# Zero-padding short matrix products to 128 rows in two attention blocks and a decay branch

## The chip, the cores and the metric

The kernel runs on one core of one Trainium2 chip. The metric is the device time of one execution in microseconds. The kernel before takes 2192.56 us, the median of three runs (2187.98 to 2196.63).

A core has a matrix engine (TensorE, PE in the profile; its weight loads have a row of their own, PEld), a vector engine (VectorE, DVE), an engine for activation functions and copies (ScalarE, ACT), GpSimd (POOL), and a queue engine (SyncE, SP) that issues the transfers. A matrix product takes a stationary operand (the weights, loaded first) and a moving one. Both lie with the contracted index on up to 128 partitions; "rows" below are these partitions. In the profile's `64*128 64x512`, 64 rows are contracted into 128 outputs, for 512 columns.

## The reference, cut to what matters

Two transformer blocks run over 256 tokens of width 1024. Each has a mixing part and an expert part (PEER: every token picks experts by two lists of 128 keys, and the kernel computes all 16384 of them densely and weighs them). The mixing part of the first block is windowed attention (8 query heads of 64 over 2 key heads, with 256 context tokens) beside a short convolution:

```
s_loc = einsum('bnqhgd,bnkhd->bhgnqk', qb, kb) * scale
s_ctx = einsum('bnqhgd,bchd->bhgnqc', qb, k_ctx) * scale
p = softmax(concatenate([s_loc, s_ctx, sink_l]))
```

The second block puts 16 meta tokens before the 256. It has latent attention, whose scores are the sum of a part of 128 dimensions and a rotary part of 64, and beside it a gated linear attention with a decay for each key dimension:

```
s = einsum('bqhd,bkhd->bhqk', qn, k_nope) + einsum('bqhd,bkd->bhqk', qp, k_pe)   # 128 and 64 dimensions
out = einsum('bhqk,bkhd->bqhd', w, v)                                           # keys: 256 tokens and 16 meta
log_a = log_sigmoid(ga @ w_a2 + b_a) / 16                                       # ga: rank 16
o = decayed causal attention of gq, gk, gv over the same 272 positions
```

## The kernel before, in words

Activations lie transposed, features on the partitions and tokens in the columns. A large product is computed in three passes (`mm3`, L177 to L179) of operands split into a high and a low part (type F32R): high by high, low by high, high by low. The 512 KB weight tiles come in one stream in the order of use: SyncE loads a raw tile (L48), ScalarE casts it to the high part (L67), VectorE subtracts to the low part (L70), TensorE uses both. Small products of attention and norms take plain F32 operands; the trace shows each as two passes ("x2").

The order is that of the Python code. Short pieces of work are generators; each time a weight tile's product has been written, every generator goes one step further, so the pieces of an attention unit stand between the plain products, a tile or more apart. Each engine runs its own list in order and waits on semaphores of the others.

The products that the change touches are these. Block 1's `attend` (L522, eight units of 128 queries, two key heads each): the scores' first product (L526) has 128 rows, the query's high part in one half of the partitions and its low part in the other, against the key's high part in both; the second (L527) takes the 64 rows of the query's high part against the key's low part `kl`. Block 2's `attend` (L1368, eight heads): each of three score blocks (272, 16 and 128 columns) is a product of 128 rows (L1377) and one of 64 (L1378); then the values are summed over keys in products of 128 rows (L1413), and over a third chunk of 48 rows that holds the meta tokens (L1414). `gla_head` (L1498, four heads): products of 128 rows (L1502, L1504) and between them one of 16 for the meta tokens (L1503). `decay` (L1263, four heads): one product of 16 rows with `wa2` (L1267).

Buffers come from pools; a tile with a tag shares its buffers with the others of the tag in turn. Opening block 2's pool reuses the memory of the expert stage before it.

Of the kernel before, what the change touches and what calls it, by code (L numbers as in the profile page):

```python
# [21 lines left out]
T = 256  # L22
META = 16
# [95 lines left out]
class Build:  # L119
# [215 lines left out]
    def block1_pre(self):  # L335
        tc, nc, A, const, spawn = self.tc, self.nc, self.A, self.const, self.spawn
        with ExitStack() as es:
# [114 lines left out]
            kh = pool.tile([128, 2, 2 * T], F32R, name="kh")  # L452
            kl = pool.tile([128, 2 * T], F32R, name="kl")
            both = ((0, slice(0, 64), slice(64, 128)), (1, slice(64, 128), slice(0, 64)))
            kT = pool.tile([128, T], F32, name="kT")
            vT = pool.tile([128, 2 * T], F32, name="vT")
            v = pool.tile([128, 4, 128], F32, name="v")
# [31 lines left out]
            def key(half, k):  # L489
                ks = slice(half * T, half * T + T)  # L490
                if not half:
                    yield from rotate(kT, k)
                    k = kT
                    yield
                for g, own, other in both:
                    nc.scalar.copy(kh[own, g, ks], k[own])
                    nc.scalar.copy(kh[other, g, ks], k[own])
                yield
                for g, own, other in both:
                    nc.vector.tensor_sub(kl[own, ks], k[own], kh[own, g, ks].bitcast(F32))  # L500

# [20 lines left out]
            def attend(b, qt):  # L522
                ts = slice(qt * 128, qt * 128 + 128)
                S = ps.tile([128, 2, 512], F32, name="S", tag="S", bufs=1)
                for g, own, other in both:
                    nc.tensor.matmul(S[:, g, :], qs[:, b, g, ts], kh[:, g, :], start=True, stop=False)  # L526
                    nc.tensor.matmul(S[:, g, :], qs[own, b, g, ts], kl[own, :], start=False, stop=True)  # L527
                yield
# [622 lines left out]
    def block2_pre(self):  # L1151
        tc, nc, A, const, spawn = self.tc, self.nc, self.A, self.const, self.spawn
        with ExitStack() as es:
# [7 lines left out]
            nh = pool.tile([128, KC, L2], F32R, name="nh")  # L1161
            nl = pool.tile([128, KC, L2], F32R, name="nl")
            wa2 = pool.tile([128, 512], F32, name="wa2")
            nc.sync.dma_start(wa2[64:80, :], A["w_a2"])
            rope = self.load("rope2", pool)
# [90 lines left out]
            kp = pool.tile([128, L2], F32, name="kp")  # L1256
            kpe = pool.tile([128, L2], F32, name="kpe")
            la = pool.tile([128, 4 * L2], F32, name="la")
# [4 lines left out]
            def decay():  # L1263

                for h in range(4):
                    pl = bank("pla", "hd")
                    nc.tensor.matmul(pl[:, :L2], wa2[64:80, h * 128:h * 128 + 128], kp[64:80, :], start=True, stop=True)  # L1267
                    yield
                    nc.scalar.activation(lat[:, h, :], pl[:, :T], AF.Identity, bias=gb_a[:, h:h + 1])
                    nc.scalar.activation(lam[:, h, :], pl[:, T:L2], AF.Identity, bias=gb_a[:, h:h + 1])  # L1270
                    yield
                for a in range(0, 4 * L2, 2 * L2):
                    a, b = la[:, a:a + 2 * L2], lb[:, a:a + 2 * L2]
                    nc.vector.scalar_tensor_tensor(b, a, -1.0, a, op0=ALU.mult, op1=ALU.min)
                    yield
                    nc.scalar.activation(b, b, AF.Exp)
                    yield
                    nc.scalar.activation(b, b, AF.Ln, bias=1.0)
                    yield
                    nc.vector.scalar_tensor_tensor(a, a, 0.0, b, op0=ALU.min, op1=ALU.subtract)  # L1280
                    nc.vector.tensor_scalar(a, a, 1.0 / 16, None, op0=ALU.mult)
                ready[0] = True
# [22 lines left out]
            def key_rope(s):  # L1305

                p = bank("pkd", "hd"), bank("pkr", "mm", 3)
                nc.tensor.matmul(p[0][:, :L2], dup[:64, :], s, start=True, stop=True)
                nc.tensor.matmul(p[1][:, :L2], rotd, s, start=True, stop=True)
                yield  # L1310
                t = pool.tile([128, L2], F32, name="kr", tag="rh", bufs=3)
                nc.vector.tensor_mul(kpe, p[0][:, :L2], rope[:, 0, :])
                nc.vector.tensor_mul(t, p[1][:, :L2], rope[:, 1, :])
                nc.vector.tensor_add(kpe, kpe, t)

# [37 lines left out]
            nc.scalar.copy(kp, mm("kpe", 0, nh, nl, L2))  # L1353
            s1 = pool.tile([64, L2], F32, name="s1")

# [7 lines left out]

            PMs = [pool.tile([48, 2, 128], F32, name="PM%d" % q) for q in range(2)]
            for t in PMs:
                nc.vector.memset(t, 0.0)

            def attend(h):  # L1368


                gs = slice(h % 2 * 64, h % 2 * 64 + 64)
                parts = (slice(288, 432), slice(0, 272))
                S = bank("S2", "S", 2)
                for q, o, ks in ((1, slice(0, 272), slice(0, L2)), (0, slice(288, 304), slice(T, L2)),
                                 (0, slice(304, 432), slice(0, 128))):
                    qs = slice(q * 128, q * 128 + 128)
                    nc.tensor.matmul(S[:, o], qT[:, h, qs], kT[:, h, ks], start=True, stop=False)  # L1377
                    nc.tensor.matmul(S[:, o], qT[gs, 8 + h // 2, qs], kpe[gs, ks], start=False, stop=True)  # L1378
                yield
# [30 lines left out]
                for q, chunks in ((0, ((0, 0),)), (1, ((0, 1), (1, 2)))):  # L1410
                    oq = o[:, q * 128:q * 128 + 128]
                    for j, (c, w) in enumerate(chunks):
                        nc.tensor.matmul(oq, v[:, c, hs], PT[:, w, :], start=j == 0, stop=False)  # L1413
                    nc.tensor.matmul(oq, v[:48, 2, hs], PM[:, q, :], start=False, stop=True)  # L1414
                yield
# [5 lines left out]
                           for a, b in ((0, 1024), (1024, 1536), (1536, 2560)))  # L1421
            AM = AM[:META]
            own = (AT[:, :, 0:128], AT1)
# [17 lines left out]
            def gla():  # L1441

                for tt in range(2):
                    nc.vector.memset(own[tt], 0.0)
                while not ready[0]:
                    yield
# [37 lines left out]
                for hp in range(2):  # L1484
                    nc.scalar.copy(AM[:, 2 * hp:2 * hp + 2, :], p[hp])
                while left[0]:
# [11 lines left out]
            def gla_head(h, o, bh):  # L1498
                p = bank("pgo", "S", 2).rearrange("p (e t) -> p e t", e=2)
                for e in range(2):  # L1500
                    vs = slice(h * 256 + e * 128, h * 256 + e * 128 + 128)
                    nc.tensor.matmul(p[:, e, :], gv[:, 0, vs], AT[:, h, :], start=True, stop=False)  # L1502
                    nc.tensor.matmul(p[:, e, :], gv[:META, 2, vs], AM[:, h, :], start=False, stop=False)  # L1503
                    nc.tensor.matmul(p[:, e, 128:], gv[:, 1, vs], AT1[:, h, :], start=False, stop=True)  # L1504
# [26 lines left out]
            for n, (kind, i) in enumerate(self.mixed):  # L1531
# [19 lines left out]
                elif kind == "ukv":  # L1551
                    if i == 0:
                        kT = pool.tile([128, 8, L2], F32, name="kT2")
                        v = pool.tile([128, 3, 1024], F32, name="v2")
                    for j in range(4 * i, 4 * i + 4):
                        p = mm("ukv", j, ckh, ckl, L2, 2, 4)
# [180 lines left out]
```

## Time and profile before

| | |
|---|---|
| median of three runs | 2192.56 us |
| profiled execution, its own time | 2196.02 us |
| its span, first to last instruction | 2194.0 us |
| TensorE busy | 2156.2 us (98%), 15318 products |
| weight loads busy | 1970.3 us (90%) |
| VectorE busy | 1585.6 us (72%) |
| ScalarE busy | 1289.5 us (59%) |
| GpSimd busy | 0.2 us, 4 instructions |
| transfers | 386.49 MB, mean 176 GB/s |
| mean granted TensorE clock | 0.997 of full speed |

The two mixing parts take 0 to 250 and about 1050 to 1395 us, the two expert parts the rest. Products are pipelined and their ends are modelled, so that durations overlap: the time that a product costs is the distance from its start to the start of the next one. A busy TensorE is therefore not a TensorE at its peak, and the table alone does not tell it.

### The profile page before, as it was taken

What the parts mean: (1) busy time and instruction counts of PE and PEld (TensorE: products, weight loads), DVE (VectorE), ACT (ScalarE), POOL (GpSimd) and SP (SyncE); (2) the same over time, 40 slices, a digit from 0 to 9 for tenths busy, and PEclk for the clock granted to TensorE, in tenths of its full rate; (3) what the DMA queues carried; (4) which work ended last, traced back from release to release, by engine and by line L of the source; (5) the groups of instructions that cost most, each with busy time, mean ns of one, the idle gap of its engine ahead of it and who ended that gap; (6) DMA issues with size and microseconds to landing.
All of it is one profiled execution on the core that took longest, in us unless ns stands there. A gap on an engine that the chain in (4) does not pass through costs nothing.

```text
span 2194.0 us, 39324 instructions
## 1 busy us (share of the span) xinstructions
PE 2156.2 (98%) x15318; PEld 1970.3 (90%) x15318; DVE 1585.6 (72%) x3063; ACT 1289.5 (59%) x2480; POOL 0.2 (0%) x4
## 2 busy tenths in 40 slices
PE   6999999999999999999999999999999999999999
PEld 3999899999999888888888889999999999888887
DVE  5786699988887555665775546699988897555555
ACT  6565554568887444444675456554568886544443
POOL 0000000000000000000000000000000000000000
PEclk9999999999999999999999999999999999999999
DMA  8576656655555666776443235566665556666665
GB/s 261 156 246 194 197 170 184 188 178 156 158 159 170 188 193 194 214 232 204 153 131 96 87 116 164 158 178 197 182 178 160 155 156 181 186 194 195 193 192 154
DMA packets 108155, 386.49 MB, mean 176 GB/s; under 512 B 12784, under 2 KB 14128, under 8 KB 107712
## 3 DMA queue, kind: packets, MB, share of 16 engines
q1 hardware_dynamic: 107968, 383.98, 58.0%
q8 instruction: 120, 1.97, 0.4%
q14 instruction: 67, 0.55, 0.1%
HBM read 382.88 MB, written 1.05 MB: 175 GB/s over the span
## 4 chain that ended last, share of the span: by engine, by line
PE 92%; DVE 3%; ACT 3%; DMA 1%; issue 1%; SPq 0%; ACTq 0%; DVEq 0%
PE acc L730 32%; PE pu L177 12%; PE pu L179 12%; PE pu L178 12%; PE pz L177 5%; PE pz L179 4%; PE pz L178 4%; PE pg L1029 3%; DVE wlo L70 1%; ACT whi L67 1%; PE pa L1433 1%; PE sp L1077 1%; PE po L565 1%; PE S L1378 1%; PE pu L224 1%
## 5 line engine op out<-in xcount | busy, mean ns | idle before, releaser
L70 DVE TENSOR_TENSOR wlo<-raw,whi 128x1024 fp32r<-128x1024 f32 x690 | 841.4, 1220 | 439.5 <-ACT whi L67 434.8
L67 ACT CAST whi<-raw 128x1024 fp32r<-128x1024 f32 x690 | 722.6, 1048 | 404.4 <-PE acc L730 347.7
L177 PE MATMUL pu<-hh,whi 128*128 128x256 f32 x2272 | 649.3, 286 | 0.0
L179 PE MATMUL pu<-hh,wlo 128*128 128x256 f32 x2272 | 635.9, 280 | 0.3
L178 PE MATMUL pu<-hl,whi 128*128 128x256 f32 x2272 | 635.6, 280 | 0.0
L178 PEld LDWEIGHTS pu<-hl,whi 128*128 128x128 f32 x2272 | 431.2, 190 | 0.0
L179 PEld LDWEIGHTS pu<-hh,wlo 128*128 128x128 f32 x2272 | 429.1, 189 | 1.1 <-DVE wlo L70 1.1
L177 PEld LDWEIGHTS pu<-hh,whi 128*128 128x128 f32 x2272 | 426.7, 188 | 0.0
L730 PE MATMUL acc<-whi,ch 128*128 128x512 f32 x1024 | 317.2, 390 | 0.0
L730 PE MATMUL acc<-whi,cl 128*128 128x512 f32 x1024 | 316.7, 389 | 0.0
L730 PE MATMUL acc<-wlo,ch 128*128 128x512 f32 x1024 | 316.6, 389 | 0.0
L730 PEld LDWEIGHTS acc<-whi,cl 128*128 128x128 f32 x1024 | 192.2, 188 | 40.1
L730 PEld LDWEIGHTS acc<-wlo,ch 128*128 128x128 f32 x1024 | 192.2, 188 | 39.8
L730 PEld LDWEIGHTS acc<-whi,ch 128*128 128x128 f32 x1024 | 191.6, 188 | 39.3
L1116 ACT ACTIVATE cb<-pu 128x256 f32<-128x256 f32 (+32 forms) x250 | 81.9, 328 | 163.6 <-PE pu L179 163.4
L1013 ACT ACTIVATE w<-oi,lists 128x128 f16<-128x128 f16 x512 | 170.3, 442 | 1.9 <-DVE oi L1007 1.4
L1021 DVE TENSOR_TENSOR cb<-cb,pg 128x248 f32<-128x248 f32 (+42 forms) x128 | 69.7, 544 | 60.7 <-ACT cb L1116 60.7
L706 DVE TENSOR_TENSOR cl<-cb,ch 128x256 fp32r<-128x256 f32 x256 | 96.6, 419 | 5.2 <-ACT ch L704 5.2
L177 PE MATMUL pz<-nh,whi 128*128 128x256 f32 (+1 forms) x328 | 97.0, 296 | 0.0
L179 PE MATMUL pz<-nh,wlo 128*128 128x256 f32 (+1 forms) x328 | 93.2, 284 | 0.0
L178 PE MATMUL pz<-nl,whi 128*128 128x256 f32 (+1 forms) x328 | 92.9, 283 | 0.0
L1114 ACT ACTIVATE gl<-pu 128x4 f32<-128x4 f32 (+21 forms) x132 | 37.3, 283 | 79.6 <-ACT w L1013 67.3
(420 smaller groups left out, 2892.9 us busy)
## 6 DMA issues: line engine op xcount, KB each, us to landing
raw<-u SPq DMA_DIRECT2D x256, 512.0 KB, 3.6
raw<-v SPq DMA_DIRECT2D x256, 512.0 KB, 3.6
raw<-w_mod_b SPq DMA_DIRECT2D x32, 512.0 KB, 4.1
raw<-pw_q SPq DMA_DIRECT2D x32, 512.0 KB, 3.9
raw<-w_in_z SPq DMA_DIRECT2D x28, 512.0 KB, 4.0
raw<-w_mod_a SPq DMA_DIRECT2D x16, 512.0 KB, 5.1
raw<-w_mix_out SPq DMA_DIRECT2D x8, 512.0 KB, 4.0
raw<-w_gv SPq DMA_DIRECT2D x8, 512.0 KB, 3.6
```

What stands on the lines that cost most here:

```text
L67: nc.scalar.copy(hi[:, :f], t[:, :f])
L70: nc.vector.tensor_sub(lo[:, :f], t[:, :f], hi[:, :f].bitcast(F32)), self.load_to(k + self.raw_bufs))
L177: self.nc.tensor.matmul(out, sh, mh, start=first and i == 0, stop=False)
L178: self.nc.tensor.matmul(out, sh, ml, start=False, stop=False)
L179: self.nc.tensor.matmul(out, sl, mh, start=False, stop=last and i == n - 1)
L706: nc.vector.tensor_sub(l[r], c[:, r, :], h[:, r, :].bitcast(F32))
L730: nc.tensor.matmul(acc[tt][dh], st[:, ts], mv[:, dh * 512:dh * 512 + 512], start=i == n == 0, stop=i == 127 and n == 2, skip_group_check=True)
L1013: nc.scalar.activation(w[:, 0, j // 2, :, j % 2], oi[:, j // 2, :, j % 2], AF.Copy, scale=gates[:, t0 + j:t0 + j + 1])
L1021: nc.vector.tensor_tensor(c[:, :n, :], c[:, :n, :], pk[:, :n, :], op=ALU.mult)
L1029: nc.tensor.matmul(p[:, j, :], oj[:, j // 2, :, j % 2], w[:, q, j // 2, :, j % 2], start=q == 0, stop=q == 1)
L1114: nc.scalar.activation(t[:, :n], p[:, :n], AF.Gelu)
L1116: nc.scalar.activation(row[:, n:], p[:, n:], AF.Gelu)
```

## The change

The named products get 128 rows on both sides, the added rows zeros on at least one of them and finite numbers on the other. No product is added and none has more columns.

- `kl` gets a slot for each key head, with zeros in the other head's 64 partitions, and L527 takes all of `qs`.
- `kpe`, block 2's rotary key, gets two such slots; VectorE writes it in two additions of 64 rows from a temporary.
- `v` and `gv` get zeros in their third chunk before the rows of the meta tokens are written, and `PM` and `AM` have 128 partitions of which the unused ones are zero.
- `wa2` is filled with zeros before its 16 rows are loaded; L1267 takes all rows of it and of `kp`.
- The zero fills are GpSimd's, but for `PM`, which VectorE fills as before.
- To make room `vT` shares the buffers of `PT`, and `s1` those of `vt`.

```diff
-            kl = pool.tile([128, 2 * T], F32R, name="kl")
+            kl = pool.tile([128, 2, 2 * T], F32R, name="kl")
+            for g in range(2):
+                nc.gpsimd.memset(kl[64 - 64 * g:128 - 64 * g, g, :].bitcast(F32), 0.0)
-            vT = pool.tile([128, 2 * T], F32, name="vT")
+            vT = pool.tile([128, 2 * T], F32, name="vT", tag="PT", bufs=2)
-                    nc.vector.tensor_sub(kl[own, ks], k[own], kh[own, g, ks].bitcast(F32))
+                    nc.vector.tensor_sub(kl[own, g, ks], k[own], kh[own, g, ks].bitcast(F32))
-                    nc.tensor.matmul(S[:, g, :], qs[own, b, g, ts], kl[own, :], start=False, stop=True)
+                    nc.tensor.matmul(S[:, g, :], qs[:, b, g, ts], kl[:, g, :], start=False, stop=True)
             wa2 = pool.tile([128, 512], F32, name="wa2")
+            nc.gpsimd.memset(wa2, 0.0)
             nc.sync.dma_start(wa2[64:80, :], A["w_a2"])
-            kpe = pool.tile([128, L2], F32, name="kpe")
+            kpe = pool.tile([128, 2, L2], F32, name="kpe")
+            gv2 = gv[:, 2, :]
+            nc.gpsimd.memset(gv2, 0.0)
+            nc.gpsimd.memset(kpe, 0.0)
-                    nc.tensor.matmul(pl[:, :L2], wa2[64:80, h * 128:h * 128 + 128], kp[64:80, :], start=True, stop=True)
+                    nc.tensor.matmul(pl[:, :L2], wa2[:, h * 128:h * 128 + 128], kp, start=True, stop=True)
-                nc.vector.tensor_mul(kpe, p[0][:, :L2], rope[:, 0, :])
+                u = pool.tile([128, L2], F32, name="ku", tag="rh", bufs=3)
+                nc.vector.tensor_mul(u, p[0][:, :L2], rope[:, 0, :])
                 nc.vector.tensor_mul(t, p[1][:, :L2], rope[:, 1, :])
-                nc.vector.tensor_add(kpe, kpe, t)
+                for g in range(2):
+                    gs = slice(g * 64, g * 64 + 64)
+                    nc.vector.tensor_add(kpe[gs, g, :], u[gs], t[gs])
-            s1 = pool.tile([64, L2], F32, name="s1")
+            s1 = pool.tile([64, L2], F32, name="s1", tag="vt", bufs=2)
-            PMs = [pool.tile([48, 2, 128], F32, name="PM%d" % q) for q in range(2)]
+            PMs = [pool.tile([128, 2, 128], F32, name="PM%d" % q) for q in range(2)]
-                    nc.tensor.matmul(S[:, o], qT[gs, 8 + h // 2, qs], kpe[gs, ks], start=False, stop=True)
+                    nc.tensor.matmul(S[:, o], qT[:, 8 + h // 2, qs], kpe[:, h % 2, ks], start=False, stop=True)
-                    nc.tensor.matmul(oq, v[:48, 2, hs], PM[:, q, :], start=False, stop=True)
+                    nc.tensor.matmul(oq, v[:, 2, hs], PM[:, q, :], start=False, stop=True)
-            AM = AM[:META]
+                nc.gpsimd.memset(AM, 0.0)
-                    nc.scalar.copy(AM[:, 2 * hp:2 * hp + 2, :], p[hp])
+                    nc.scalar.copy(AM[:META, 2 * hp:2 * hp + 2, :], p[hp])
-                    nc.tensor.matmul(p[:, e, :], gv[:META, 2, vs], AM[:, h, :], start=False, stop=False)
+                    nc.tensor.matmul(p[:, e, :], gv[:, 2, vs], AM[:, h, :], start=False, stop=False)
                         v = pool.tile([128, 3, 1024], F32, name="v2")
+                        nc.gpsimd.memset(v[:, 2, :], 0.0)
```

TensorE's list keeps its order. What moves is the filling. GpSimd's whole list behind the start of the program reads, in the changed kernel (`wa` is `wa2`, and `at` the buffer that holds AM):

```order
L455 MEMSET kl 64x512 x2
L1167 MEMSET wa_12065 128x512 [waits DMAHW4_49,DMAHW5_49,DMAHW3_49,DMAHW6_49,DMAHW0_49,DMAHW7_49,PE_49,Pool_49]
L1263 MEMSET gv 128x1024
L1264 MEMSET kpe 128x544
L1564 MEMSET v_12968 128x1024 [waits DVE_49]
L1453 MEMSET at 128x1024 [waits DVE_49,PE_49,Activation_49]
L1742 UNCONDITIONAL_BRANCH
```

None of these seven fills was there before.

SyncE's list at the opening of block 2's pool, before (from the first of two weight tiles of the latent key, `w_ckv`, on to the tables of block 2):

```order
L48 DMA raw<-w_ckv 128x1024 [waits DMAHW3_49,DVE_49]
L1164 DMA wa_12063<-w_a 16x512 [waits PE_49]
L144 DMA rope_12065<-rope 128x544
L144 DMA dup_12067<-dup 128x128
L144 DMA rot_12069<-rot 128x128
```

and the same place in the changed kernel:

```order
L48 DMA raw<-w_ckv 128x1024 [waits DMAHW3_49,DVE_49]
L1168 DMA wa_12065<-w_a 16x512 [waits Pool_49]
L144 DMA rope_12068<-rope 128x544
L144 DMA dup_12070<-dup 128x128
L144 DMA rot_12072<-rot 128x128
```

The load of `w_a` waited for TensorE's last use of the memory; now it waits for GpSimd's fill, which waits for TensorE. Three more tables and the second tile of `w_ckv` follow in both, in the same order.

## Rows read from the trace of the kernel before

**Rows 1.** The page: chain by engine; splits of weight tiles (busy, mean ns).
```profile
PE 92%; DVE 3%; ACT 3%; DMA 1%; issue 1%; SPq 0%; ACTq 0%; DVEq 0%
...
L70 DVE TENSOR_TENSOR wlo<-raw,whi 128x1024 fp32r<-128x1024 f32 x690 | 841.4, 1220 | 439.5 <-ACT whi L67 434.8
L67 ACT CAST whi<-raw 128x1024 fp32r<-128x1024 f32 x690 | 722.6, 1048 | 404.4 <-PE acc L730 347.7
```

**Rows 2.** Stages: length, busy of PE, PEld, DVE, ACT, POOL; clock; DMA share, GB/s.
```profile
95.00:207.00 112.00, 111.76 (x884) 101.37 (x883) 84.64 (x142) 68.98 (x135) 0.00 (x0) 1.00 0.68 218
...
1160.00:1290.00 130.00, 128.97 (x942) 115.04 (x941) 77.04 (x170) 62.81 (x159) 0.00 (x0) 1.00 0.31 96
```

**Rows 3.** Waits of PE, 90 to 207 and 1160 to 1290: us, times, longest.
```profile
PE S L526 <- ACT P L541: 0.2, 1, 0.2
...
PE pz L177 <- ACT gv L1337: 0.9, 1, 0.9
```

**Rows 4.** Timeline, PE, first unit of block 1's attention: start, duration (us).
```profile
97.36 0.28 PE L179 MATMUL pz<-h1h,wlo 128*128 128x256 f32 x1
97.47 0.40 PE L526 MATMUL S<-kh,qs 128*128 128x512 f32 x1
97.80 0.49 PE L527 MATMUL S<-kl,qs 64*128 64x512 f32 x1
...
99.07 0.39 PE L177 MATMUL pz<-h1h,whi 128*128 128x256 f32 x1
99.30 0.28 PE L178 MATMUL pz<-h1l,whi 128*128 128x256 f32 x1
```

**Rows 5.** Timeline, PEld, same place; in brackets idle time before and its releaser.
```profile
97.80 0.18 PEld L527 LDWEIGHTS S<-kl,qs 64*128 64x128 f32 x1 [0.25 <-issue]
...
99.30 0.19 PEld L179 LDWEIGHTS pz<-h1h,wlo 128*128 128x128 f32 x1
```

**Rows 6.** Chain in order of time: start, us, passes (256, 16, 512, 128 columns).
```profile
51.37 3.72 PE pst L205 x16
...
746.33 1.69 PE pstm L205 x16
748.02 266.66 PE acc L730 x1176
...
1157.66 1.78 PE pa L1433 x16
```

**Rows 7.** Timeline, PE, first head's scores in block 2, with the next products.
```profile
1162.88 0.62 PE L1377 MATMUL S<-kT,qT 128*128 128x272 f32 x2
...
1165.80 0.29 PE L178 MATMUL pz<-ckl,whi 128*128 128x272 f32 x1
```

**Rows 8.** Timeline, PE, a head's values in block 2, to the next scores.
```profile
1191.64 0.38 PE L1413 MATMUL po<-PT,v 128*128 128x128 f32 x2
...
1193.81 0.62 PE L1377 MATMUL S<-kT,qT 128*128 128x272 f32 x2
```

**Rows 9.** Timeline, PE, first head of the decay branch's output.
```profile
1292.35 0.59 PE L1502 MATMUL pgo<-at,gv 128*128 128x256 f32 x2
...
1295.42 0.28 PE L178 MATMUL pz<-hl,whi 128*128 128x256 f32 x1
```

**Rows 10.** Timeline, PE, first gate product of the decay, with its neighbours.
```profile
1111.07 0.59 PE L1295 MATMUL pb<-sqh,one 128*128 128x256 f32 x2
...
1112.47 0.28 PE L178 MATMUL pz<-hl,whi 128*128 128x256 f32 x1
```

**Rows 11.** Timeline, SP, second tile of w_ckv.
```profile
1065.91 0.37 SPq L48 DMA_DIRECT2D raw<-w_ckv  x1
```

**Rows 12.** DMA issues, 1047 to 1110 us: count, KB, median us to landing.
```profile
raw<-w_ckv SPq DMA_DIRECT2D x2, 512.0 KB, 5.2
```

**Rows 13.** Timeline, PE, first product of that tile.
```profile
1078.91 0.47 PE L177 MATMUL pz<-nh,whi 128*128 128x272 f32 x1
```

**Rows 14.** Line L1444, VectorE's zero fills: ns min/median/max, starts, shape.
```profile
L1444 DVE MEMSET at<- x2: 485/485/485, 1151.0 to 1151.6; 128x512 f32 x2
```

More of the change, by code (lines that the diff above doesn't have):

```diff
@@ L1368, in attend @@
             def attend(h):
-                gs = slice(h % 2 * 64, h % 2 * 64 + 64)
                 parts = (slice(288, 432), slice(0, 272))
```

## The prediction

> **What bounds the kernel now.** I read the chain of waits first: 92% of it is TensorE, and nothing on it is a transfer worth speaking of (DMA 1%) [rows 1]. Then I cut the span into stages and looked at the two in which the change sits. In block 1's attention (95 to 207 us) TensorE is busy 111.8 of 112 us, VectorE 84.6, ScalarE 69.0; in block 2's (1160 to 1290 us) 129.0 of 130, 77.0 and 62.8; the granted clock is 1.00 in both, the 2.4 GHz level [rows 2]. The list of waits in the same two stretches has one line each for TensorE, 0.2 and 0.9 us [rows 3]. So a microsecond taken from TensorE's stream there is, to first order, a microsecond of the kernel.
>
> Busy time does not say whether TensorE does useful work, so I went on to the order of time. In the first attention unit, products of 256 columns stand 0.11 us apart (97.36, 97.47). Then come four products of 512 columns, with 128, 64, 128 and 64 rows, and 97.47 to 99.07 is 1.60 us for them, 0.40 each; the first plain product behind them holds its place for 0.23 instead of 0.11 [rows 4]. 1176 products of 512 columns in the expert stage take 266.66 us, 0.227 each [rows 6]. The missing 0.17 is seen in the weight loads: between 128-row products a load of 0.19 us lies under the product before; at 97.80 the loader has been idle for 0.25 us with nothing to wait for ("issue"), and load and product start together [rows 4, 5]. So each change of the row count, in either direction, lays one weight load open.
>
> **The change part by part.** It gives 128 rows to every product that had fewer in five places. No product is added and none gets more columns, so I cost what is left by what 128-row neighbours take. An F32 instruction shows as two passes (x2); per pass 128 rows cost 0.106 us at 16 columns (1.69/16), 0.111 at 128 (1.78/16) and 0.233 at 256 (3.72/16), which makes 0.247 at 272 by columns [rows 6]. F32R products run in one pass: 0.227 at 512, half of it, 0.113, at 256, and 0.12 at 272.
>
> - Scores of block 1 (L526, L527; 8 units, 4 changes each). Now 97.47 to 99.30, 1.83 us, with the first product behind [rows 4]. Then 4 x 0.227 + 0.113 = 1.02. Gain 0.81, eight times: 6.5 us.
> - Scores of block 2 (L1377, L1378; 8 units, 6 changes). Now 1162.88 to 1165.80, 2.92 us [rows 7]. Then four passes each at 272, 16 and 128 columns, 0.99 + 0.42 + 0.44, and 0.12 for the product behind: 1.97. Gain 0.95, eight times: 7.6 us.
> - Values of block 2 (L1413, L1414; 8 units, 4 changes). Now 1191.64 to 1193.81, 2.17 us with the three transposes behind [rows 8]. Then 13 passes of 128 columns, 1.44. Gain 0.73, eight times: 5.8 us.
> - The decay branch's output (L1502 to L1504; 4 heads, 4 changes). Now 1292.35 to 1295.42, 3.07 us [rows 9]. Then eight passes of 256 and four of 128 columns and one product: 1.86 + 0.44 + 0.11 = 2.42. Gain 0.65, four times: 2.6 us.
> - The decay's gate product (L1267; 4 heads, 2 changes). Now 1111.07 to 1112.47, 1.40 us, for a sum (two passes of 256), the product (two of 272) and one product behind [rows 10]. Then 0.47 + 0.49 + 0.11 = 1.07. Gain 0.33, four times: 1.3 us.
>
> Together 23.8 us for 136 changes, 0.175 each. The bound above is the whole idle time of 0.25 us at each change [rows 5], 34 us; it counts the 0.04 us for which the loader rests anyway between products of 512 columns (0.227 less 0.19), so I keep the measured sequences.
>
> What is given back. The second unit's scores need the bank that the first unit's exponentials read, and TensorE already waits 0.2 us for them [rows 3]: that wait is set by VectorE and ScalarE, so the first unit's 0.8 us is lost. With each gain TensorE comes nearer to the exponentials of the later units too, so I take off as much again, 0.8. In block 2 the 0.9 us wait for an evacuation stays [rows 3], and I take off 0.5 for others like it. 23.8 - 2.1 = 21.7 us.
>
> What is added. Seven zero fills on GpSimd, which had next to nothing before: no row has such a fill, and the nearest is VectorE's of 128x512, 0.485 us [rows 14]. Below nothing it can't be, since it is new work on a path that had none. Six of them are wanted late: their readers stand tens of microseconds behind. The one with something queued behind is the fill of wa2: SyncE's load into it now waits for GpSimd, and behind that load stand the tables and the next weight tile. At present that tile issues at 1065.91 and TensorE takes it up at 1078.91, 13.0 us later; of these, landing takes 5.2 (a median), the cast 1.05 and the subtraction 1.22 [rows 1, 11 to 13], which leaves 5.5 us. At VectorE's price the fill delays SyncE by some 0.5 us, at four times this by 2: both are covered, and I take 0. VectorE's one more addition in the key rotation (half the rows twice instead of all once, some 0.4 us) and the shared buffers (vT with PT, s1 with vt, a third user of rh) cost at most one late release of about 0.5 us; I take 0 there too.
>
> The profiled execution took 2196.02 us around a span of 2194.0; 21.7 less is 2174.3. The median of the runs lies 3.5 lower, at 2192.56, and the forecast for it is 2170.9, say **2171 us**.
>
> Page and trace differ on one point. In the trace loads of 128x128 weights follow each other every 0.11 to 0.12 us although each takes 0.19 [rows 4, 5], so they overlap the products, all on the same 128 rows. The Trainium skill (TensorE: Matmul & The Clock Gate, Part 3, The mechanism) says that a weight load runs under a product in flight only when the two use different row groups. By that rule products that all have 128 rows would lay every load open, the change would give nothing, and the sum would be 0 instead of 21.7; the trace bears it out only where the row counts differ, the opposite case, so I give it a small chance below.
>
> **The rivals.**
> *The other engines take over.* TensorE gets ahead and finds exponentials, masks or weight splits late. For it: the 0.2 us wait, and VectorE's load of 76% in block 1, which becomes 84.6/105.5 = 80%. Against: TensorE's waits come to 0.2 and 0.9 us in two stretches of 112 and 130 us [rows 2, 3], and in block 2 VectorE goes only from 59% to 77/116 = 66%. If block 1 gave nothing and block 2 half, 17.3/2 = 8.7 us would be left: 2184.
> *The loads stay open.* What costs the time would then be the load itself behind an operand of another tile or type, and not the row count: nothing gained, 2192.6. For it: the first product behind an F32 product sometimes holds its place longer too, without a change of rows. Against: the loader's idle time stands at each change, and the expert stage changes its operands all the time at 0.227.
> *SyncE is held by GpSimd.* The fill of wa2 has to end before SyncE goes on. It costs from 5.5 us on, and from 5.5 + 21.7 = 27.2 us the kernel is slower. A fill of 40 us, eighty times VectorE's, would give 2192.6 - 21.7 + 34.5 = 2205. For it: the queue does stand behind it, and GpSimd's price is unknown. Against: the factor.
>
> **How the numbers follow.** Forecast 0.85, other engines 0.08, loads stay open 0.04, SyncE held 0.03. A measurement of this kernel tells about 0.5%, 11 us, from no change. The forecast lies 21.7 us under the median and is faster in all of its own range (2163 to 2178: the 34 us bound less the 2.1 would be 2161, and 14 us gained 2178). Other engines: 0.03 of it faster, 0.05 within. Open loads: within. So faster 0.88, same 0.09, slower 0.03. The range for 8 in 10 takes the upper bound of the gain and a part of the first rival: 2160 to 2180.
>
> **What would show it.** In the changed kernel's order of time, block 1's four score products should stand 0.23 us apart, the twelve score passes of block 2 with the product behind take about 2.0 us, a decay head 2.4; the "issue" idle time of the weight loader at these lines should be gone. The stretch from the first scores to the first product of the second expert stage should be shorter by some 20 us, and the two expert stages the same. GpSimd's fill of wa2 should end before 1068 us on the old scale. Wrong it would be if the starts close up and TensorE's waits for ScalarE or VectorE grow by as much, or if the 128-row products keep starting with their loads.

## The result, and the profile after

The changed kernel takes 2165.88 us, the median of four runs (2165.46 to 2172.54), against 2190.32 us (2187.98 to 2196.63, four runs) of the kernel before: ratio 0.9887, 95% interval 0.9868 to 0.9906, 24.4 us less between the medians and 22.5 between the lowest runs. The forecast was 2171 us and 21.7 us less, its range 2160 to 2180. Measured once more, six runs of it gave 2165.05 to 2174.05 against 2187.78 to 2196.09 of the kernel before, ratio 0.9900 (0.9883 to 0.9917).

The page's chain of the changed kernel still reads as [rows 1]:

```profile
PE 92%; DVE 3%; ACT 3%; issue 1%; DMA 1%; SPq 0%; ACTq 0%; DVEq 0%
```

The order of time on TensorE, in block 1's first unit of scores (start, duration, then the instruction):

```profile
96.58 0.28 PE L179 MATMUL pz<-h1h,wlo 128*128 128x256 f32 x1
96.70 0.39 PE L528 MATMUL S<-kh,qs 128*128 128x512 f32 x1
96.93 0.39 PE L529 MATMUL S<-kl,qs 128*128 128x512 f32 x1
97.16 0.40 PE L528 MATMUL S<-kh,qs 128*128 128x512 f32 x1
97.40 0.40 PE L529 MATMUL S<-kl,qs 128*128 128x512 f32 x1
97.64 0.28 PE L177 MATMUL pz<-h1h,whi 128*128 128x256 f32 x1
97.75 0.28 PE L178 MATMUL pz<-h1l,whi 128*128 128x256 f32 x1
```

The four products stand 0.23 to 0.24 us apart, and from the first of them to the second plain product it is 1.05 us; it was 1.83 [rows 4]. The weight loads beside them, in the row PEld of the same stretch, have no idle time before them, where the loader sat idle for 0.25 us and then loaded with the product waiting [rows 5]:

```profile
96.93 0.19 PEld L528 LDWEIGHTS S<-kh,qs 128*128 128x128 f32 x1
97.17 0.19 PEld L529 LDWEIGHTS S<-kl,qs 128*128 128x128 f32 x1
```

Each of these loads begins with the product before the one that it serves. The other four places, in TensorE's order of time: the decay's gate product with its sum (1098.30), one head's scores in block 2, the fourth's (1187.86; the first head's take the same within 0.01 us), a head's values (1253.19), and the first head of the decay's output (1265.52), each with the row at which it is over:

```profile
1098.30 0.59 PE L1302 MATMUL pb<-sqh,one 128*128 128x256 f32 x2
...
1099.31 0.28 PE L178 MATMUL pz<-hl,whi 128*128 128x256 f32 x1
...
1187.86 0.62 PE L1386 MATMUL S<-kT,qT 128*128 128x272 f32 x2
...
1189.79 0.28 PE L178 MATMUL pz<-nl,whi 128*128 128x256 f32 x1
...
1253.19 0.39 PE L1422 MATMUL po<-PT,v 128*128 128x128 f32 x2
...
1254.31 1.06 PE L1441 MATMUL pa<-gq,gk 128*128 128x128 f32 x8
...
1265.52 0.59 PE L1511 MATMUL pgo<-at,gv 128*128 128x256 f32 x2
...
1267.81 0.28 PE L178 MATMUL pz<-hl,whi 128*128 128x256 f32 x1
```

That is 1.01 for the gate product (1.40 in [rows 10]), 1.93 for a head's scores (2.92 in [rows 7]), 1.12 for the ten passes of the values (with three more at 0.11, as [rows 8] has them, 1.45 against 2.17), and 2.29 for a decay head (3.07 in [rows 9]).

What was given back in block 1 stands in TensorE's waits, in the stretch from 90 to 207 us (total, times, longest):

```profile
PE S L528 <- ACT P L543: 1.0, 1, 1.0
```

The 0.2 us of [rows 3] have become 1.0: the 0.8 us of the first unit, lost at the second. The stages around the change (length; busy of PE, PEld, DVE, ACT and POOL; granted clock; DMA share; GB/s), which answer to [rows 2], are nearly as full as before, with VectorE no closer to its end than 79% and 66%:

```profile
94.23:199.90 105.67, 104.67 (x875) 100.49 (x874) 83.77 (x140) 68.57 (x134) 0.00 (x0) 1.00 0.70 230
1136.00:1250.00 114.00, 111.89 (x909) 109.16 (x908) 75.29 (x171) 62.57 (x172) 0.00 (x0) 1.00 0.35 103
```

GpSimd's fill of `wa2`, from its order of time, and then SyncE's load behind it and the second tile of `w_ckv`, which answers to [rows 11]:

```profile
1047.36 0.54 POOL L1167 MEMSET wa<- 128x512 f32 x1 [1045.54 <-PE pf L205]
```

```profile
1049.50 0.42 SPq L1168 DMA_DIRECT2D wa<-w_a  x1
...
1053.14 0.37 SPq L48 DMA_DIRECT2D raw<-w_ckv  x1
```

The fill is over before SyncE gets there. The tile issues 12.77 us earlier than in [rows 11], and the last products of the expert stage ahead of it came earlier by the same 12.77 (1037.34 instead of 1050.11). The fill delays nothing.

The profiled execution of the kernel before was a long one (2196.02), so I read the differences by stages, in this table from the chain of each kernel's profile and, for the first scores, from its order of time. The first stage goes from block 1's first scores to the first product of the first experts (`pu`), the others on from there, to the experts' first long run of `acc`, to the first product of the second experts, and to their `acc`:

| kernel | block 1 | first experts, to `acc` | `acc` and block 2 | second experts, to `acc` |
|---|---|---|---|---|
| before | 152.68 | 449.92 | 695.13 | 444.97 |
| before, once more | 153.84 | 443.79 | 695.09 | 444.92 |
| after | 147.36 | 443.26 | 677.83 | 444.48 |
| after, once more | 146.97 | 443.17 | 677.63 | 444.80 |
| block 1 alone | 148.72 | 443.79 | 695.08 | 449.59 |
| block 2 and decay alone | 153.95 | 443.18 | 677.85 | 449.79 |
| grouped, not padded | 149.89 | 443.24 | 685.81 | 444.50 |
| wa2 filled 64 times | 148.58 | 443.27 | 708.39 | 444.84 |
| wa2 filled 8 times | 146.94 | 448.13 | 677.85 | 445.01 |
| after, values interleaved | 145.93 | 443.30 | 677.56 | 449.79 |
| the same, once more | 145.31 | 443.20 | 677.82 | 444.66 |

The change is worth 5.3 us in block 1 and 17.3 in block 2 between the two profiles first compared. An expert stage, which the change does not touch, takes 443 to 445 us or 448 to 450, in either place and with or without the change. Of the 6.7 us of the first one some 5 are of that kind. The other 1.6 are the clock's: the stage's first 32 products take 5.57 us there and 3.97 in the changed kernel, in a stretch whose granted clock is 0.66 (columns as in [rows 2]), where the changed kernel has 1.00:

```profile
250.15:255.15 5.00, 5.00 (x29) 5.00 (x30) 5.00 (x12) 3.80 (x8) 0.00 (x0) 0.66 0.00 0
```

### The profile page after: what moved, and what is told of

It reads as the page before. It is cut to its first block, busy times and chain, and to the rows that moved or that the text cites. A ratio compares the mean times of both kernels' runs of the same rounds, so it can differ in the third digit from the quotient of the medians.

```text
span 2163.4 us, 39342 instructions
## 1 busy us (share of the span) xinstructions
PE 2123.7 (98%) x15318; PEld 1961.8 (91%) x15318; DVE 1584.4 (73%) x3064; ACT 1289.0 (60%) x2480; POOL 5.1 (0%) x11
## 3 DMA queue, kind: packets, MB, share of 16 engines
HBM read 382.88 MB, written 1.05 MB: 177 GB/s over the span
## 4 chain that ended last, share of the span: by engine, by line
PE 92%; DVE 3%; ACT 3%; issue 1%; DMA 1%; SPq 0%; ACTq 0%; DVEq 0%
PE acc L732 32%; PE pu L177 12%; PE pu L179 12%; PE pu L178 12%; PE pz L177 4%; PE pz L179 4%; PE pz L178 4%; PE pg L1031 3%; DVE wlo L70 1%; ACT whi L67 1%; DMA raw<-w_mod_a 1%; PE pa L1441 1%; PE sp L1079 1%; PE po L567 1%; PE pu L224 0%
## 5 line engine op out<-in xcount | busy, mean ns | idle before, releaser
L1116 ACT ACTIVATE gl<-pu 128x4 f32<-128x4 f32 (+21 forms) x132 | 37.3, 283 | 79.9 <-ACT w L1015 67.6
```

The lines of the kernel that those rows point to most:

```text
L1116: nc.scalar.activation(t[:, :n], p[:, :n], AF.Gelu)
```

## The experiments

**The order alone.** The kernel before with products of one row count put side by side, so that 136 changes become 64; nothing is padded. In block 2 and the decay the sums that share a bank then stand open side by side and are not all kept; instructions and shapes are those of before.

```diff
                 for g, own, other in both:
                     nc.tensor.matmul(S[:, g, :], qs[:, b, g, ts], kh[:, g, :], start=True, stop=False)
+                for g, own, other in both:
                     nc.tensor.matmul(S[:, g, :], qs[own, b, g, ts], kl[own, :], start=False, stop=True)
...
```

> The kernel before, no row added: only the order inside a unit differs. Block 1's scores take both 128-row products and then both 64-row ones; block 2's scores three and three; the values and the decay heads likewise, short ones last. The 136 changes of the row count become 64 (16+16+16+8+8). Theory (a change of the row count lays one weight load open, some 0.175 us): 72 changes fewer, 12.5 us, less about 0.5 given back: 2178 beside 2190. In the order of time a head's scores in block 2 take 2.92 - 4 x 0.16 = 2.3 us. If the step from the lower 64 rows to the upper 64 in block 1 counts as a change too, 1.4 us less gain. Rival (a product of few rows is slow by itself, whatever stands beside it): no gain, 2190, and 2.9 us for a head's scores.

Measured: 2175.15 us (2173.24 to 2175.83) against 2192.33 (2188.34 to 2195.64), ratio 0.9917 (0.9904 to 0.9931). The gain between the lowest runs is 15.1 us, where 12 were expected; the stages of its profile gain 2.8 and 9.3, 12.1 together, and a head's scores in block 2 take 2.32 us, where 2.3 were expected. The rival's 2190 and 2.9 are out. The first unit, TensorE's order of time:

```profile
96.62 0.63 PE L526 MATMUL S<-kh,qs 128*128 128x512 f32 x2
97.17 0.50 PE L528 MATMUL S<-kl,qs 64*128 64x512 f32 x2
97.60 0.39 PE L177 MATMUL pz<-h1h,whi 128*128 128x256 f32 x1
97.83 0.28 PE L178 MATMUL pz<-h1l,whi 128*128 128x256 f32 x1
```

The two products of 64 rows together take 0.43 us with two changes in it, so that the second adds next to nothing: they use the lower and the upper 64 rows and run side by side, which the next but one experiment shows by itself. The unit takes 1.21 us, 0.62 less, of which, as an estimate from the streams below, the two changes gone make 0.40 and the pair side by side the rest. So the cost goes with the change of the row count, and not with having fewer rows.

**Block 1 alone.** The kernel before with the padded `kl` and the shared buffer of `vT`, nothing else.

```diff
-                    nc.tensor.matmul(S[:, g, :], qs[own, b, g, ts], kl[own, :], start=False, stop=True)
+                    nc.tensor.matmul(S[:, g, :], qs[:, b, g, ts], kl[:, g, :], start=False, stop=True)
...
```

> The kernel before with block 1's part of the change alone (kl in two slots, vT beside PT). Theory: 32 changes go, 6.5 us by the sequences, 4.9 after what the prediction takes off (the second unit waits longer for the first one's exponentials): 2185 beside 2190; the stretch from the first score product to the first product of the expert stage 5 us shorter than in the kernel before. Rival (VectorE and ScalarE, 76% and 62% busy there, take the gain back): that stretch as before, and waits of TensorE for them of several us.

Measured: 2184.91 us (2183.15 to 2190.09), ratio 0.9964 (0.9950 to 0.9978), 5.2 us between the lowest runs. Its block-2 stage keeps its 695.08 us. The waits are the changed kernel's, 1.0 us at the second unit and nothing behind it. Its block-1 stage is 4.0 us shorter than in the first profile of the kernel before and 5.1 than in the second, where 5 were expected. In it the clock falls behind the attention, where the changed kernel keeps 1.00, and that costs some 1.5 us; first this kernel, then the changed one (columns as in [rows 2]):

```profile
217.37:231.15 13.78, 13.78 (x106) 13.78 (x105) 11.38 (x13) 7.52 (x13) 0.00 (x0) 0.88 0.73 232
217.11:229.36 12.25, 12.25 (x105) 12.25 (x105) 10.25 (x13) 6.08 (x12) 0.00 (x0) 1.00 0.77 241
```

**Pairs of products by themselves.** A kernel that computes nothing of the reference: streams of 24 products on loaded tiles, each stream with one pattern of shapes, and no waits in between.

```diff
+        for i in range(N):  # 128 and the lower 64
+            r = (slice(0, 128), lo)[i % 2]
+            mm(B(i, r), wr[r, st(i)], xr[r, 0:512])
...
```

> Not the reference's computation: streams of 24 products each out of two loaded operands, the output is not computed. One stretch for each pattern, read by the distance from start to start. Theory: 128 rows alone 0.22 to 0.23 us at 512 columns; 128 and 64 in turn 0.40 (a load of 0.18 laid open each time); 64 alone 0.22 to 0.23, as the 128; 128 and 48, 128 and 16 in turn 0.40 like 64; at 256 columns the same 0.17 to 0.18 on top of 0.113; F32 with 128 columns 0.22 for both passes, 0.40 with changes. Rival (few rows are slow by themselves): 64 alone 0.40. Open, no forecast: lower and upper 64 in turn, 128 and 96, 64 and 48, and outputs of 128 and 64 in turn.

Its stretches (length; busy and number of PE, PEld, ACT and POOL; granted clock; DMA share; GB/s), one in each stream, all of TensorE's 512-column products first: 128 rows alone, 128 and 64 in turn, 64 alone, lower and upper 64 in turn, 128 and 96, 128 and 48, the same further on; at the lower clock level 128 and 16 in turn, and 128 and 64 in turn at 256 columns; then F32 passes of 128 columns: outputs of 128 and 64 in turn, outputs to the lower and upper 64 in turn, 128 rows alone, 128 and 64 rows in turn:

```profile
20.00:25.00 5.00, 5.00 (x24) 4.14 (x23) 0.00 (x0) 0.00 (x0) 1.00 0.00 0
26.00:34.00 8.00, 8.00 (x20) 3.45 (x19) 0.00 (x0) 0.00 (x0) 1.00 0.01 2
35.50:40.00 4.50, 4.50 (x21) 3.65 (x20) 0.00 (x0) 0.00 (x0) 1.00 0.00 0
40.30:43.00 2.70, 2.70 (x26) 2.21 (x24) 0.00 (x0) 0.00 (x0) 1.00 0.00 0
44.00:49.00 5.00, 5.00 (x23) 4.05 (x22) 0.00 (x0) 0.00 (x0) 1.00 0.00 0
50.00:54.00 4.00, 4.00 (x11) 1.80 (x10) 0.00 (x0) 0.00 (x0) 1.00 0.00 0
55.00:62.00 7.00, 7.00 (x11) 2.63 (x10) 0.00 (x0) 0.00 (x0) 0.50 0.00 0
...
72.00:88.00 16.00, 16.00 (x24) 6.26 (x22) 0.00 (x0) 0.00 (x0) 0.50 0.00 0
90.00:98.00 8.00, 8.00 (x17) 4.37 (x16) 0.00 (x0) 0.00 (x0) 0.50 0.00 0
...
107.50:115.50 8.00, 8.00 (x43) 4.96 (x41) 0.00 (x0) 0.00 (x0) 1.00 0.00 0
116.50:118.50 2.00, 2.00 (x41) 2.00 (x38) 0.00 (x0) 0.00 (x0) 1.00 0.03 8
119.50:124.00 4.50, 4.50 (x43) 4.50 (x42) 0.00 (x0) 0.00 (x0) 1.00 0.00 0
125.00:133.50 8.50, 8.50 (x42) 6.06 (x42) 0.62 (x2) 0.00 (x0) 1.00 0.00 0
```

A stretch counts a product or two that only reach into it; from start to start it is 0.227 us for 128 rows alone and for 64 alone, and 0.427 for the two in turn, where 0.40 was expected. One change costs 0.20 us, and the loader's busy share falls from 83 to 43%. The rival's 0.40 for 64 rows alone is out. With 96 rows there is next to none of the cost (0.235), with 48 it is all there (0.427). F32 passes of 128 columns take 0.111 us alone and 0.21 with 128 and 64 rows in turn, as expected. Lower and upper 64 rows in turn, on different banks, come two in 0.227 us.

The forecasts for 16 rows and for 256 columns are not tested at the higher clock level, since the clock had fallen. At the lower level a change costs some 0.30 us: products with 128 and 16 rows in turn stand 0.72 apart, and 64 and 48 in turn, which show no such cost, 0.427; at 256 columns it is 0.51 with 128 and 64 rows in turn and 0.213 with 128 alone.

The output's width counts too: outputs of 128 and 64 in turn take 0.195 us a pass against 0.111. Outputs to the lower and upper 64 in turn take 0.055.

Each product of a stream loads other weights than the one before it, and at the five places of the changed kernel tiles and types change with no load laid open, so that "the loads stay open" is out.

**A long fill ahead of SyncE's load.** The changed kernel with the fill of `wa2` done 64 times.

```diff
-            nc.gpsimd.memset(wa2, 0.0)
+            for _ in range(64):
+                nc.gpsimd.memset(wa2, 0.0)
```

> The changed kernel with the zero fill of wa2 done 64 times over, so that SyncE waits for it some 27 us longer (64 x 0.46 us from 1047.4 on, where SyncE stands there at 1049.5). The prediction's price for that queue: 5.5 us covered, the rest shows, 22 us: 2188 beside the changed kernel's 2166. Rival (the tiles behind are wanted so late that it is covered): 2166.

Measured: 2197.11 us, and the block-2 stage is 30.6 us longer than the changed kernel's. GpSimd and SyncE in order of time, TensorE's longest wait, and the stretch behind it (columns as in [rows 2]):

```profile
1048.39 37.31 POOL L1168 MEMSET wa<- 128x512 f32 x64 [1046.56 <-PE pf L205]
```

```profile
1085.73 0.34 SPq L1169 DMA_DIRECT2D wa<-w_a  x1
```

```profile
PE pstl L205 <- ACT sql L1233: 28.5, 1, 28.5
```

```profile
1094.00:1104.00 10.00, 8.46 (x43) 8.20 (x44) 4.70 (x5) 6.40 (x12) 0.00 (x0) 0.64 0.77 263
```

A fill takes 0.58 us in such a row. The load issues 35.2 us later than in the changed kernel (36.2, less 1.0 by which the whole stage lies later), and TensorE, waiting for the second tile of `w_ckv` by way of its squares, loses 28.5: 6.7 us are covered. The other 2.1 come behind the wait, when the products run at the lower clock level (0.23 us apart instead of 0.13) until about 1101 us. The 2188 expected was 9 us too low: the load came 35.2 us late and not 27, 1.2 us more of that were covered, and the 2.1 behind the wait were left out. So what the prediction's rival of a held SyncE describes is real, and in the changed kernel it costs nothing only because the one fill is short.

**Eight fills.** The same with 8 in place of 64.

> The changed kernel with the zero fill of wa2 done 8 times over. With 64 fills, 0.58 us each in the trace, SyncE's load of wa2 came 35 us late and TensorE waited 28.5 us: 6.7 us of the delay were covered. Theory (cover of 5.5 to 6.7 us, then a price of one for one): 8 fills delay the load by about 3 us, all covered, so 2166 as the changed kernel, and TensorE has no wait of over 1 us in the stretch behind the first expert stage. Rival (every delay of SyncE's queue is paid): about 3 to 4 us slower, with a wait of TensorE of that size there.

Measured: 2170.95 us, 5 over the changed kernel. But the block-2 stage is 677.85 us, as in the changed kernel, and TensorE's waits there are the same. SyncE:

```profile
1057.09 0.34 SPq L1169 DMA_DIRECT2D wa<-w_a  x1
...
1061.41 0.37 SPq L48 DMA_DIRECT2D raw<-w_ckv  x1
```

By this stage's place (5.1 us later than in the changed kernel) the load issues 2.5 us late and the tile 3.2: both covered. The 5 us stand in the first expert stage (448.13), ahead of the fill.

**The kernel before, once more.** No edit.

> The kernel before, unchanged, profiled once more: where do the 6.7 us of the first expert stage come from? Theory: they belong to the execution that was profiled, not to the change. A stage of this kernel has two courses: products of 256 columns 0.118 apart over some 130 us, or 0.113. The padded block 1 alone showed the slow course in its second expert stage. Then either stage here takes 443 to 445 us in the fast course and 450 in the slow one, and the span is about 2187 if both are fast. Rival: the slow course of the first stage is a property of the old block 1 in front of it; then the first stage takes 450 us again and the span is 2194 again. A second slow first stage would not decide between them, a fast one would.

Measured: 2190.45 us, span 2188.4, its first expert stage 443.79 us. The long stage did not come back, so it is not the old block 1 that makes it. Where the time is, in this profile, and below it in the profile first taken (columns as in [rows 2]):

```profile
300.82:350.82 50.00, 50.00 (x442) 50.00 (x441) 47.04 (x167) 26.05 (x39) 0.00 (x0) 1.00 0.63 181
350.82:400.82 50.00, 50.00 (x444) 50.00 (x443) 49.56 (x174) 23.79 (x36) 0.00 (x0) 1.00 0.64 193
```

```profile
300.15:350.15 50.00, 50.00 (x429) 50.00 (x429) 45.98 (x162) 25.60 (x39) 0.00 (x0) 1.00 0.61 178
350.15:400.15 50.00, 50.00 (x427) 50.00 (x426) 48.25 (x167) 22.92 (x37) 0.00 (x0) 1.00 0.63 188
```

In the long course 427 products are started in 50 us, 0.117 apart, in the short one 444, 0.113, at the same granted clock, with VectorE and ScalarE a little less busy. What sets the course stays open. The stage is 6.1 us shorter than in the first profile, 1.6 of it the clock's at its start, as said above. Against this profile the changed kernel's span is 25.0 us shorter: 6.5 in block 1, 17.3 in block 2, 1.2 elsewhere. The 1.2 us by which block 1 is longer here than in the first profile are the clock's, at the fifth unit's scores, here and, in the second fence, in the first profile:

```profile
146.00:150.50 4.50, 4.50 (x18) 3.33 (x18) 3.62 (x8) 1.48 (x3) 0.00 (x0) 0.64 0.91 338
```

```profile
146.48:150.98 4.50, 4.50 (x29) 3.53 (x29) 2.59 (x4) 2.29 (x3) 0.00 (x0) 1.00 0.94 297
```

**Block 2 and the decay alone.** The changed kernel without its part in block 1.

```diff
-                    nc.tensor.matmul(S[:, g, :], qs[:, b, g, ts], kl[:, g, :], start=False, stop=True)
+                    nc.tensor.matmul(S[:, g, :], qs[own, b, g, ts], kl[own, :], start=False, stop=True)
...
```

> The change without its part in block 1 (the scores' kl and the buffer of vT): only block 2's attention and the decay branch have 128 rows. Theory (each part is worth its own laid-open loads, and the parts add up): 7.6 + 5.8 + 2.6 + 1.3 = 17.3, less the 0.5 given back, 16.8 us, so about 2175 if the kernel before is at 2192; the stretch between the expert stages 16 to 18 us shorter than before, the stretch of block 1 at its 152.7 us. Rival (the parts lean on each other, a shorter block 1 is needed for the later stretches to move): 8 us or less, 2184.

Measured: 2174.88 us (2174.39 to 2176.87), ratio 0.9922 (0.9904 to 0.9940), its block-2 stage 677.85 us, 17.3 less than before, and block 1 not shorter than before (153.95). The two parts lower the ratio by 0.36 and 0.78%, 1.14 together, and the whole change by 1.13: the parts add up. Between the lowest runs this part makes 14.1 us; its profile has a long second expert stage (449.79), and whether its other runs had one too is not known.

**Values interleaved.** The stream of outputs to the lower and upper half pointed to a place that the change leaves alone: block 1's values, 16 passes of 64 output columns a unit.

```diff
-                for g in range(2):
-                    for j in range(4):
+                for j in range(4):
+                    for g in range(2):
...
```

> The changed kernel, with the 16 passes of block 1's values (64 output columns: the two groups write the lower and the upper 64 rows of one bank) in the order lower, upper, lower, upper instead of eight lower and then eight upper. In the stream of products alone, passes of 64 output columns that go to the lower and upper half in turn stood 0.055 us apart. In the changed kernel they stand 1.51/16 = 0.094 apart. Theory (two halves of the array run side by side): 16 x 0.039 = 0.6 us less for each of 8 units, 5.0 us, less what the exponentials give back: 2161 to 2163, and 16 passes in about 0.9 us. Rival (in the kernel the passes are held by their weight loads, of 64 columns and 0.09 us, in either order): 2166, and 1.5 us for 16 passes.

Measured: 2163.16 us (2162.54 to 2169.42), ratio 0.9869 (0.9850 to 0.9887). The group of these products (busy, mean ns of one, idle before), here and in the changed kernel:

```profile
L567 PE MATMUL po<-PT,v 128*64 128x128 f32 x128 | 8.8, 279 | 0.0
```

```profile
L567 PE MATMUL po<-PT,v 128*64 128x128 f32 x128 | 12.7, 279 | 0.0
```

3.9 us less, where 5.0 were forecast: 16 passes take 1.02 us in place of 1.51. Pairs in the middle stand 0.109 apart, as in the stream, and the changes of columns at both ends stay (0.16 and 0.20 us). The rival's 1.5 us is out; its weight loads of 64 columns take 0.13 to 0.14 us in these traces and not 0.09. TensorE's wait for the exponentials grows from 1.0 to 1.7. To compare the two on one chip, both once more:

> The changed kernel once more, beside the version with interleaved values on the same chip. 2166 (2165.5 to 2166 in most runs), ratio to the kernel before 0.989; its second profile should have the block-1 units 9.1 to 13.8 us apart as in the first, and any difference between its span and the first's 2163.4 in the first or the second expert stage (443 to 445 us or 448 to 450).

> The changed kernel with the interleaved values of block 1, beside the changed kernel on the same chip. Theory (0.49 us less for each of 8 units, in the trace of its first run, less 0.7 us that TensorE waits longer for the exponentials): 3 us under the changed kernel, 2163. Rival (the first run's 2.7 us lay between two chips): the same as the changed kernel, within 0.5 us.

Measured: the changed kernel 2169.07 us (2165.05 to 2174.05; three of its six runs at 2165 to 2167, the others at 2171 to 2174, where I had expected most at 2166), the interleaved 2163.62 (2162.22 to 2168.27), ratios 0.9900 and 0.9877 (0.9858 to 0.9895). The lowest runs are 2.8 us apart; the intervals of the ratios overlap. In this pair of profiles the last unit's values begin 2.8 us earlier after the first scores, but the block-1 stage is only 1.7 us shorter: in both profiles of the interleaved kernel the clock falls behind the attention as it did in block 1 alone (a mean of 0.94 over the last 29 us before the experts), and in neither of the changed kernel's. It is the fastest kernel of this study, and how much of the gain is left is not settled by these runs.

## Why the prediction was right, point by point

*The reason held.* A change of the row count lays one weight load open, and equal row counts hide it: the loader's idle time is gone at 128 rows, grouping by itself takes away 72 of the 136 changes and brings 12.1 of the 22.6 us by the stages, and in a stream with nothing else in it a change costs 0.20 us. The forecast said 0.175, the mean over the kernel's five places; measured there it is 0.18 (24.6 us for 136).

*The terms.* Scores of block 1: 0.78 a unit (0.81 said), 6.2 us. Scores of block 2: 0.99 a head (0.95), 7.9. Values: 0.72 (0.73), 5.8. Decay heads: 0.78 (0.65), 3.1. Gate: 0.39 (0.33), 1.6. That is 24.6 us against 23.8; the two short terms were a little low because F32 passes of 256 columns took 0.22 us there and not the 0.233 of [rows 6].

*What is given back.* The first unit's 0.8 us were lost as said. The second 0.8, for the exponentials of later units, was not: from the second unit's wait on, the units start as much earlier as TensorE saves (the last three, 12.77 and 9.90 us apart in the second profile of before, are 12.00 and 9.11 apart). 5.4 is left, 5.3 measured, 4.9 said. In block 2 the terms make 18.4 and the stage gained 17.3, so 1.1 came back where 0.5 was said; the list of waits shows about half of it, as new waits of 0.3 and 0.4 us at a transpose and a rotation, less 0.2 that is gone. Where the rest went is not shown. So the 2.1 us taken off and the 1.9 measured agree in part by luck: 0.8 too much in block 1, 0.6 too little in block 2. Together 22.7 where 21.7 was said, and 22.5 to 22.7 between the lowest runs.

*The fills.* Nothing, as said. The cover was 6.7 us and not 5.5, and beyond it the price is more than one for one, for the clock falls in the wait. The 37.3 us of 64 fills cost 30.6, so that the rival's 40 us would cost some 33, where it said 34.5.

*The distance of 5 us to the median.* 1 us is the terms above. 2.2 are the base: the forecast went from one median of three runs, 2192.56, and beside the changed kernel the kernel before had 2190.32. The other 1.8 lie in the spread: the medians are 24.4 us apart, the lowest runs 22.5 and the stages 22.6. The runs of the kernel before spread over 9 us; between its two profiles, 5.6 us apart, the first expert stage alone makes 6.1.

*The stretch as a whole.* From the first scores to the second experts it was to be some 20 us shorter, and the expert stages the same. It is 29.3 shorter than in the first profile of before and 24.3 than in the second; 6.7 and 0.5 of that are the first expert stage.

*The rivals.* Other engines: one wait longer by 0.8 us, and waits longer by 0.5 in block 2, no more. Loads that stay open: no. The Trainium skill (TensorE: Matmul & The Clock Gate, Part 3, The mechanism) says in its list that loads overlap only where the row groups differ, though the same section names the background weight buffer as another way; here they overlap among products that all have 128 rows, and lie open where the row count changes between 128 and 64, 48 or 16. There the measurement decides against the rule of the list. Another page of the Trainium skill (TensorEngine Tiling (Array Packing), Tiling Modes, Key Properties) says that a change of the tiling mode, and not just of the tile, drains TensorE, and that different tiles load and multiply in parallel. The streams agree with both, at 0.20 us a change and at two products of lower and upper 64 rows in 0.227 us, though a trace shows only the load that starts late and not the drain itself.

## What to carry to other kernels

Read the starts on the matrix engine, not its busy time: where a product takes 0.17 to 0.20 us more than its columns ask for and the weight loader idles in "issue" ahead of it, look whether the shape of the product before it was another. Then give all of them one shape, with zeros, or put those of one shape side by side, and pairs that use different halves next to each other. Before a fill goes to an idle engine, count the cover at the queue that will wait for it.

## What was not expected

- The clock fell in a stream of products with TensorE busy throughout. In the stream of 128 and 48 rows in turn the granted clock was 1.00 from 50 to 54 us and 0.50 (1.2 GHz) from 55 to 62, with no wait, and the loader busy for 45% and 38%; by 106 us, behind products of 128 rows alone, it was at 1.00 again. In the kernel, two of three profiles with the old block 1 show it at the fifth unit's scores (0.64 and 0.71 over 4.5 us, the third 1.00), some 1.5 us each; none of those with a padded or grouped block 1 does. But in five of these eight (block 1 alone, grouped, both interleaved, 64 fills) it fell further on, at 214 to 222 us, behind a wait of 1.6 us and one of 0.6 that the others have too, and with the loader busy throughout (13.78 of 13.78 us in block 1 alone). So a fall needs no open loads at its place, and whether they make one more likely is not shown.
- 96 rows go with 128 (0.235 us in turn) and 48 with 64 rather than with 128 (0.427): here not every change of the row count costs.
- Whole expert stages run some 5 us (1%) longer in some executions, 0.117 us between products and not 0.113, at a granted clock of 1.00.
